# Start of a two-layer trunk: squares added by VectorE, projections in other PSUM banks, sinks on VectorE, modulation strips in front of their pair

## The chip, the cores and the metric

The kernel runs on one core of one Trainium2 chip. The time is the device time of one execution in microseconds (us). The kernel before was run three times: 1536.33, 1536.4 and 1539.2 us, median 1536.4 us. One further execution was profiled.

## The reference, cut to what matters

Two layers (DEPTH = 2) of a transformer-like trunk work on 512 latent tokens and 256 context tokens of width 1024. In each layer:

```python
h   = rmsnorm(x, norm1_g) * (1 + scale) + shift       # shift, scale = silu(c) @ w_mod + b_mod
z   = h @ w_in                                        # q 512, k 128, v 128, u 512, g 512 columns
q,k = rope(rmsnorm(q)), rope(rmsnorm(k))              # per head of 64; context without rope
attn = softmax(q k^T) v                               # 8 query heads, 2 key/value heads
gm   = gelu(u) * (w_spatial @ layernorm(gelu(g)) + b) # 128x128 mixing per chunk and group
x   += gate * (concat(attn, gm) @ w_out)
x   += gate * (square(relu(modulate(rmsnorm(x)) @ w_ff1)) @ w_ff2)
```

The context tokens use the same weights with a modulation of their own (c_ctx), and in the last layer only their keys and values are needed. Everything is float32 at the interface.

## The kernel before, in words

**Number format.** A float32 factor is split into a high part (rounded to the matmul type, by ScalarE, line 215) and a low part (the difference, by VectorE or GpSimd, line 216). A product takes three matmuls: high x high, high x low, low x high (`mm`, line 211). Activations are kept transposed, features on partitions, tokens along the free axis; `h0[k]` holds the high and low part of feature tile k (k = 0..7) for 768 tokens.

**Start.** `start` (lines 1183 to 1230) runs with the orders of TensorE (PE) and VectorE (DVE) written out by hand: the two engines execute its instructions in the order of the program. ScalarE (ACT) and GpSimd (POOL) are ordered by a planner before the run, and so is everything outside such a region. It works on the 512 latent tokens:

- The mean square per token: ACT squares each X[k] (line 1188), PE multiplies the 128x128 pieces of the square by a column of ones and accumulates over k (line 1192). Square tiles come from tag `s`, which has three buffers. VectorE scales, GpSimd takes the power -1/2 (line 292), VectorE spreads the result into a diagonal (`diag`, line 501), and four PE transposes turn it into a row for all partitions (`bcast`, line 506).
- Four modulation chunks (`mod_chunk`, lines 337 to 369), each in two halves of two 512 KB weight tiles and eight matmuls (line 348); here a half is called a strip. When a chunk is complete, VectorE transposes it in blocks (line 356), and its `fin` selects the rows with four matmuls (line 361) and stores shift and scale (`mod_store`, lines 421 and 424).
- For each pair of feature tiles c = 0..3: `convert` (lines 215 and 216) splits the projection weights of the pair, `pieces` (lines 494 to 496) makes `h0[2c]` and `h0[2c+1]` from X, scale, shift and the row of the norm, and `latents(k)` (line 598) multiplies them by 512 projection columns (keys, values and the first 256 queries): 12 matmuls for each k into four PSUM banks of tag `pa`. The strips of later chunks lie between and after the `latents` calls.
- The context's squares are added on GpSimd (`cx.step`, line 470); `cx.sums` stands in the middle of the last `latents` call. After `start` follow `cx.bcast()` and `cx.apply(h0)` (lines 1242 and 1243), which make the context's part of `h0`.

**DMA queue.** All weights are issued on SyncE's queue in the order of `block_order` (line 124): chunk 0, tok 0, chunk 1, tok 1, chunk 2, tok 2, chunk 3, tok 3, then the context's X and further weights. The first tiles land in buffers that are used again later (`EARLY`, line 119): chunk 2 goes where chunk 0 was, chunk 3 where chunk 1 was, so a load waits until the matmuls of the older chunk have read it.

**Projections of a layer.** `PLAN` (line 120) lists them: for layer 0 `w0` (gate u, tile 0, latent tokens), `kv` (sinks of what `start` has projected, then the context's projection in two banks of tag `pb`), `x0` (tile 0, context tokens), `u1`, then banks A0, u2, A1, A2, B0, B1, B2 (the spatial-gating part), then the second half of the queries and `u3`. `TokProj.bank` (line 553) computes 256 tokens by 256 columns: 48 matmuls into a PSUM bank, which its sink reads. PSUM has tags `pa` (two tiles of two banks), `pb` (two banks) and `pt` (two banks). The banks of `TokProj` come from `pt`, since `self.early` is true in both layers; `pt` also serves the mixing matmuls (line 853), the transposes of keys and queries (`turn`, line 724) and those of the norms.

**Sinks.** `both` (line 774) hands keys, values and first queries of 256 tokens to `sink_kv` and `sink_q`. Their `qk` (lines 678 to 707) squares on ACT, sums and multiplies by the rotary factors on VectorE, and, called with `pool` true, adds (line 696), takes the power (line 292) and multiplies (line 706) on GpSimd. `stack` (line 709) makes the low part on GpSimd in layer 0 (line 712), and `turn` transposes on PE. The gating sink `sink_g` runs gelu (lines 787 to 792), a layer norm and a mixing.

The later stages (attention, output projection, feed-forward) are not touched.

Of the kernel before, what the change touches and what calls it, by code (L numbers as in the profile page):

```python
# [15 lines left out]
D = 1024  # L16
# [152 lines left out]
def trunk(ctx: ExitStack, tc: tile.TileContext, xT, pk1, pk2, rope, wsT, w_mod, w_tok, w_u, w_out, w_ff1, w_ff2, outT):  # L169
# [57 lines left out]
    def convert():  # L227

        if held:
            split(*held.pop(0))  # L230
# [104 lines left out]
    fins = []  # L335

    def mod_chunk(l, j, lag=1200.0):
# [20 lines left out]
        def fin():  # L358
# [3 lines left out]
            mod_store(l, j, p4)  # L362
# [86 lines left out]
    class Norm:  # L449
# [22 lines left out]
        def sums(self, *others):  # L472
# [10 lines left out]
            r = rsqrt(v, o, self.l)  # L483
# [53 lines left out]
    class TokProj:  # L537
        def __init__(self, l, grp, h, npair, sink):
# [4 lines left out]
            self.early = PAR["BK"] == 1 and kv0 is None  # L543
# [122 lines left out]
    def layer(l, h, nxt, K, kv=None, kv0=0):  # L666
# [107 lines left out]
        def both(tp, ps):  # L774
            sink_kv(tp, [p[:, 0:256] for p in ps] if isinstance(ps, list) else ps[:, :, 0:256], True)
            q0(tp, [p[:, 256:512] for p in ps] if isinstance(ps, list) else ps[:, :, 256:512], True)
# [20 lines left out]
        def u_part(m, part):  # L797
# [5 lines left out]
            fm_mms(ps, w8(upart[m], h), off, n)  # L803
# [65 lines left out]
        with region('proj%d' % l):  # L869
            gproj = {}  # L870
            for s in PLAN[l]:
# [4 lines left out]
                elif s == "kv" and l == 0:  # L876
                    for tp in range(2):
                        both(tp, kv.ps[tp])
# [304 lines left out]
    def start():  # L1183
        ps = [pa() for _ in range(2)]
        chunk = [mod_chunk(0, c, None) for c in range(4)]
        for k in range(KT):
            sq = tsm([128, SEQ])
            act.activation(sq, xk(k)[:, 0:SEQ], AF.Square)
            if k == KT - 1:
                next(chunk[0])  # L1190
            for t in range(4):
                pe.matmul(ps[t // 2][:, t % 2 * 512:t % 2 * 512 + 1], sq[:, t * 128:(t + 1) * 128], ones[:, 0:1], start=k == 0, stop=k == KT - 1)  # L1192
        v = small(4)
        for i in range(2):
            vec.tensor_scalar(v[:, 2 * i:2 * i + 2], ps[i].rearrange("p (b n) -> p b n", b=2)[:, :, 0], 1.0 / D, EPS, op0=ALU.mult, op1=ALU.add)
        r = rsqrt(v, 4, 1)
        next(chunk[0])
        lat.diag(r)
# [4 lines left out]
        for c in range(4):  # L1203
            k = 2 * c
            lows = []
            if c:
                convert()
            lows.append(lat.pieces(h0, k))
# [6 lines left out]
            if c == 3:  # L1215
                convert()
                kvq.latents(k)
                kvq.latents(k + 1, cx.sums)
                break
# [3 lines left out]
            kvq.latents(k)  # L1223
            next(chunk[c + 1])
            kvq.latents(k + 1, lambda: fins.pop()())
            if c < 2:
                next(chunk[c + 2])
        P2 = K0[0]
        vec.tensor_scalar_mul(P2("bs"), P2("bs"), 0.5)
# [12 lines left out]
    cx.bcast()  # L1242
    cx.apply(h0)
# [63 lines left out]
```

## Time and profile before

| | us |
|---|---|
| median of three runs | 1536.4 |
| profiled execution, its own time | 1537.07 |
| its span | 1535.3 |
| PE busy in the span | 1478.6 (96%) |
| DVE / ACT / POOL busy | 882.3 / 638.7 / 360.8 |

The profiled execution lies 0.67 us over the median and 1.77 us over its own span. Times in the views are counted from the span's start. Engines: PE is TensorE (PEld its weight loads), DVE VectorE, ACT ScalarE, POOL GpSimd, SP SyncE. In a row of the timeline stand start, duration, engine, line, operation, output tile <- input tiles, shape, count and, in brackets, the idle time before it and what ended it. In a row of a view by stages each engine has its busy time with its count of instructions; then come the granted clock of PE (1.00 is full), the DMA share and the GB/s moved.

### The profile page before, as it was taken

What the parts mean: (1) busy time and instruction counts of PE and PEld (TensorE: products, weight loads), DVE (VectorE), ACT (ScalarE), POOL (GpSimd) and SP (SyncE); (2) the same over time, 40 slices, a digit from 0 to 9 for tenths busy, and PEclk for the clock granted to TensorE, in tenths of its full rate; (3) what the DMA queues carried; (4) which work ended last, traced back from release to release, by engine and by line L of the source; (5) the groups of instructions that cost most, each with busy time, mean ns of one, the idle gap of its engine ahead of it and who ended that gap; (6) DMA issues with size and microseconds to landing.
All of it is one profiled execution on the core that took longest, in us unless ns stands there. A gap on an engine that the chain in (4) does not pass through costs nothing.

```text
span 1535.3 us, 22099 instructions
## 1 busy us (share of the span) xinstructions
PE 1478.6 (96%) x8682; PEld 1297.0 (84%) x8682; DVE 882.3 (57%) x1593; ACT 638.7 (42%) x1081; POOL 360.8 (23%) x341
## 2 busy tenths in 40 slices
PE   7978989999999999999999999999999999999998
PEld 5668968788889898999999899898889888888887
DVE  2646676787855555444444446756795644444443
ACT  2443154665544543433333224534783433322221
POOL 0261240221244643213232303137113000000000
PEclk9999999999999999999999999998999999999999
DMA  8221164310143333333333321222101222233321
GB/s 326 95 70 54 56 233 152 112 42 15 49 129 121 117 117 117 117 105 122 110 124 113 107 69 42 77 75 69 42 1 56 97 96 96 96 96 97 99 97 65
DMA packets 50088, 148.78 MB, mean 97 GB/s; under 512 B 5440, under 2 KB 6976, under 8 KB 49984
## 3 DMA queue, kind: packets, MB, share of 16 engines
q1 hardware_dynamic: 49408, 146.72, 28.6%
q8 instruction: 68, 1.11, 0.3%
q10 hardware_dynamic: 576, 0.66, 0.1%
q14 instruction: 36, 0.29, 0.1%
HBM read 145.26 MB, written 2.10 MB: 96 GB/s over the span
## 4 chain that ended last, share of the span: by engine, by line
PE 83%; DVE 7%; ACT 4%; POOL 3%; issue 2%; DMA 1%; POOLq 0%; SPq 0%; ACTq 0%; DVEq 0%
PE pa L211 51%; PE pb L211 18%; PE pt L211 8%; PE pt L971 3%; PE pb L348 2%; POOL m L292 1%; PE pa L1192 1%; DVE lo L216 1%; PE pt L724 1%; ACT hi L215 1%; DVE A L513 1%; DVE X L911 1%; DVE s L517 1%; DVE B L1091 1%; ACT w L955 0%
## 5 line engine op out<-in xcount | busy, mean ns | idle before, releaser
L211 PE MATMUL pa<-A,hi 128*128 128x384 f32 (+2 forms) x1728 | 459.2, 348 | 3.4 <-ACT w L1084 1.0
L215 ACT CAST hi<-raw 128x1024 fp32r<-128x1024 f32 x168 | 176.5, 1051 | 450.7 <-PE pa L211 373.5
L211 PEld LDWEIGHTS pa<-A,hi 128*128 128x128 f32 x1728 | 310.7, 189 | 27.8 <-ACT w L1084 2.7
L216 DVE TENSOR_TENSOR lo<-raw,hi 128x1024 fp32r<-128x1024 f32 x152 | 194.2, 1277 | 237.3 <-ACT hi L215 233.9
L211 PE MATMUL pa<-A,lo 128*128 128x384 f32 (+2 forms) x864 | 299.2, 347 | 0.0
L211 PE MATMUL pa<-B,hi 128*128 128x512 f32 (+1 forms) x900 | 239.9, 355 | 3.6 <-DVE X L911 3.6
L394 POOL TENSOR_TENSOR C<-C,s 128x512 f32<-128x512 f32 x112 | 164.9, 1488 | 315.4 <-ACT s L393 273.5
L211 PEld LDWEIGHTS pa<-B,hi 128*128 128x128 f32 x900 | 158.8, 189 | 31.6 <-DVE X L911 5.9
L211 PEld LDWEIGHTS pa<-A,lo 128*128 128x128 f32 x864 | 162.8, 189 | 10.7
L911 DVE SCALAR_TENSOR_TENSOR X<-pa,modT,X 128x512 f32<-128x512 f32 x126 | 82.9, 660 | 141.1 <-PE pa L211 141.1
L211 PE MATMUL pb<-B,hi 128*128 128x512 f32 (+1 forms) x600 | 156.8, 350 | 2.0 <-DVE X L911 2.0
L211 PE MATMUL pa<-B,lo 128*128 128x512 f32 (+1 forms) x450 | 157.8, 355 | 0.0
L211 PE MATMUL pt<-hi,A 128*128 128x256 f32 x576 | 115.0, 297 | 8.2 <-DVE s L792 5.7
L211 PEld LDWEIGHTS pb<-B,hi 128*128 128x128 f32 x600 | 104.2, 189 | 16.5 <-DVE X L911 3.0
L911 DVE SCALAR_TENSOR_TENSOR X<-pb,modT,X 128x512 f32<-128x512 f32 (+3 forms) x116 | 71.0, 618 | 80.0 <-PE pb L211 79.7
L211 PEld LDWEIGHTS pt<-hi,A 128*128 128x128 f32 x576 | 97.0, 204 | 10.3 <-issue 7.8
L211 PE MATMUL pb<-B,lo 128*128 128x512 f32 (+1 forms) x300 | 104.6, 349 | 0.0
L393 ACT ACTIVATE s<-k,silu 128x512 f32<-128x512 f32 x112 | 76.8, 715 | 41.1 <-DMA k<-in_w_mod 31.6
L211 PEld LDWEIGHTS pa<-B,lo 128*128 128x128 f32 x450 | 84.1, 189 | 11.3
L211 PE MATMUL pt<-lo,A 128*128 128x256 f32 x288 | 84.9, 295 | 0.0
L974 DVE TENSOR_TENSOR A<-pt,A 128x384 fp32r<-128x384 f32 (+1 forms) x144 | 73.2, 535 | 10.3 <-ACT A L973 8.8
L973 ACT CAST A<-pt 128x384 fp32r<-128x384 f32 (+1 forms) x144 | 64.2, 469 | 31.0 <-PE pt L971 27.4
(195 smaller groups left out, 2242.7 us busy)
## 6 DMA issues: line engine op xcount, KB each, us to landing
raw<-in_w_ff SPq DMA_DIRECT2D x128, 512.0 KB, 3.5
k<-in_w_mod SPq DMA_DIRECT2D x96, 256.0 KB, 3.1
raw<-in_w_tok SPq DMA_DIRECT2D x16, 512.0 KB, 3.5
raw<-in_w_out SPq DMA_DIRECT2D x16, 512.0 KB, 3.5
lo<-in_w_mod SPq DMA_DIRECT2D x16, 512.0 KB, 4.7
hi<-in_w_mod SPq DMA_DIRECT2D x16, 512.0 KB, 4.4
A<-in_w_mod SPq DMA_DIRECT2D x8, 512.0 KB, 6.8
B<-in_w_mod SPq DMA_DIRECT2D x8, 512.0 KB, 7.8
```

The source lines that it names most:

```text
L211: pe.matmul(out, a, b, start=start, stop=stop)
L215: act.copy(hi, src)
L216: (eng or vec).tensor_tensor(out=lo, in0=src, in1=hi.bitcast(F32), op=ALU.subtract)
L292: pool_e.tensor_tensor(out=y, in0=v, in1=mhalf[:, 0:n], op=ALU.pow)
L348: pe.matmul(ps[q:q + 32, :], S32[:, k, :], ws_[k2 // 2][:, k2 % 2 * 512:(k2 % 2 + 1) * 512], start=k < ns, stop=k >= KT - ns)
L393: act.activation(p, w, AF.Copy, scale=s)
L394: pool_e.tensor_tensor(out=a, in0=a, in1=p, op=ALU.add)
L513: (pool_e if k % 2 < PAR['LP'].get('%d%d%d' % (l, w, off // 256), 0) else vec).scalar_tensor_tensor(out=h[k][:, 1, off:off + n], in0=t, sc ...
L911: vec.scalar_tensor_tensor(out=xs, in0=src[:, s - off:e - off], scalar=modT[l][:, i * 8 + m, cond:cond + 1], in1=xs, op0=ALU.mult, op1=ALU ...
L971: pe.transpose(tp_[:, (kt - k0) * 128:(kt - k0) * 128 + 128], p[:, kt * 128:kt * 128 + 128], ident)
L973: act.copy(pth[:, k0:k0 + step, d], src)
L974: vec.tensor_tensor(out=ptl[:, k0:k0 + step, d], in0=src, in1=pth[:, k0:k0 + step, d].bitcast(F32), op=ALU.subtract)
```

## The change

- The squares of the latent tokens are no longer multiplied by ones tile by tile. `lat.step(k)` squares on ACT and adds on VectorE; `lat.sums(pool=1)` multiplies the finished sum by ones once (four matmuls). It stands behind chunk 0, whose two strips now run one after the other (`run(chunk[0])`).
- In the loop over pairs, both strips of chunk c + 1 run directly in front of `latents(2c)` for c = 1 and 2 (chunk 1: its first strip before the loop, its second between the two `latents` of c = 0). The selecting matmuls of a chunk stand in the middle of a `latents` call of the pair before the one that uses the chunk; `mod_store` of chunks 1 to 3 is put off (`mods`) until behind the next `convert`.
- `cx.bcast()` stands inside `w0`, behind the matmuls of k = 4, in an order of PE written out by hand, and `cx.apply(h)` behind its matmuls; before, both stood in front of `w0`. The halving of the spatial bias moves behind `start`.
- `both` calls the sinks without `pool`: addition, inverse square root (nine small operations, lines 295 to 305) and product run on VectorE in layer 0. `stack` stays on GpSimd.
- `self.early` is false: the banks of `TokProj` come from `pb` in both layers.

```diff
--- before.py
+++ after.py
@@ -332,7 +332,7 @@
     modT = [const.tile([128, 48, 2], F32, name=f"modT{l}") for l in range(DEPTH)]
     Amod = [[const.tile([128, 8, 2], F32, name=f"A{l}{w}") for w in range(2)] for l in range(DEPTH)]
 
-    fins = []
+    fins, mods = [], []
 
     def mod_chunk(l, j, lag=1200.0):
 
@@ -359,7 +359,10 @@
             p4 = pt((128, 4, 2))
             for a in range(4):
                 pe.matmul(p4[a * 32:a * 32 + 32], P1("sel")[0:rows], tr[0:rows].rearrange("p (m a i) -> p a m i", m=4, a=4)[:, a, :, 0:2], start=True, stop=True)
-            mod_store(l, j, p4)
+            if l == 0 and 0 < j < 4:
+                mods.append(lambda: mod_store(l, j, p4))
+            else:
+                mod_store(l, j, p4)
         if lag is None:
             fins.append(fin)
         elif lag:
@@ -469,7 +472,7 @@
             eng = pool_e if k < 7 and PAR["NP"] & self.tagn or self is cx else vec
             eng.tensor_tensor(out=self.acc, in0=self.acc, in1=sq, op=ALU.add)
 
-        def sums(self, *others):
+        def sums(self, *others, pool=0):
 
             every = (self,) + others
             ps = pt()
@@ -480,7 +483,7 @@
                     o += 1
             v = small(o)
             vec.tensor_scalar(v, ps[:, 0:o], 1.0 / D, EPS, op0=ALU.mult, op1=ALU.add)
-            r = rsqrt(v, o, self.l)
+            r = rsqrt(v, o, self.l or pool)
             o = 0
             for a in every:
                 a.diag(r[:, o:o + a.n // 128])
@@ -540,7 +543,7 @@
             self.key = ("tok", l, grp)
             self.l, self.grp = l, grp
             self.wb = {}
-            self.early = PAR["BK"] == 1 and kv0 is None
+            self.early = False
 
         def passes(self, k):
             if k // 4 not in self.wb:
@@ -772,8 +775,8 @@
         q0 = sink_q(0)
 
         def both(tp, ps):
-            sink_kv(tp, [p[:, 0:256] for p in ps] if isinstance(ps, list) else ps[:, :, 0:256], True)
-            q0(tp, [p[:, 256:512] for p in ps] if isinstance(ps, list) else ps[:, :, 256:512], True)
+            sink_kv(tp, [p[:, 0:256] for p in ps] if isinstance(ps, list) else ps[:, :, 0:256])
+            q0(tp, [p[:, 256:512] for p in ps] if isinstance(ps, list) else ps[:, :, 256:512])
         if kv is None:
             kv = TokProj(l, 0, h, 3, None)
             kv.sink = sink_kv
@@ -800,7 +803,16 @@
             if part == 0:
                 upart[m] = take("u", l, m)
             ps = pt()[:, 0:n]
-            fm_mms(ps, w8(upart[m], h), off, n)
+            if part:
+                fm_mms(ps, w8(upart[m], h), off, n)
+            else:
+                with tc.manual_schedule(engines={mybir.EngineType.PE}):
+                    for k, (whi, wlo, rhi, rlo) in enumerate(w8(upart[m], h)):
+                        for i, (a, b) in enumerate(((whi, rhi), (whi, rlo), (wlo, rhi))):
+                            mm(ps, a, b[:, off:off + n], k == 0 and i == 0, k == KT - 1 and i == 2, n)
+                        if k == 4:
+                            cx.bcast()
+                cx.apply(h)
             if part:
                 release()
             fl.tick()
@@ -874,6 +886,7 @@
                 elif s[0] in "wx":
                     u_part(int(s[1]), "wx".index(s[0]))
                 elif s == "kv" and l == 0:
+                    vec.tensor_scalar_mul(P2("bs"), P2("bs"), 0.5)
                     for tp in range(2):
                         both(tp, kv.ps[tp])
                     both(2, kv.context())
@@ -1181,52 +1194,38 @@
             steady(range(8))
 
     def start():
-        ps = [pa() for _ in range(2)]
         chunk = [mod_chunk(0, c, None) for c in range(4)]
         for k in range(KT):
-            sq = tsm([128, SEQ])
-            act.activation(sq, xk(k)[:, 0:SEQ], AF.Square)
-            if k == KT - 1:
-                next(chunk[0])
-            for t in range(4):
-                pe.matmul(ps[t // 2][:, t % 2 * 512:t % 2 * 512 + 1], sq[:, t * 128:(t + 1) * 128], ones[:, 0:1], start=k == 0, stop=k == KT - 1)
-        v = small(4)
-        for i in range(2):
-            vec.tensor_scalar(v[:, 2 * i:2 * i + 2], ps[i].rearrange("p (b n) -> p b n", b=2)[:, :, 0], 1.0 / D, EPS, op0=ALU.mult, op1=ALU.add)
-        r = rsqrt(v, 4, 1)
-        next(chunk[0])
-        lat.diag(r)
+            lat.step(k)
+        run(chunk[0])
+        lat.sums(pool=1)
         fins.pop()()
         lat.bcast()
         next(chunk[1])
         kvq = WideProj(h0)
         for c in range(4):
             k = 2 * c
-            lows = []
             if c:
                 convert()
-            lows.append(lat.pieces(h0, k))
+                mods.pop()()
+            lows = [lat.pieces(h0, k)]
             if not c:
                 convert()
                 lows.pop()()
             lows.append(lat.pieces(h0, k + 1))
             for f in lows:
                 f()
-            if c == 3:
-                convert()
-                kvq.latents(k)
-                kvq.latents(k + 1, cx.sums)
-                break
             if c == 2:
                 for i in range(KT):
                     cx.step(i)
-            kvq.latents(k)
-            next(chunk[c + 1])
-            kvq.latents(k + 1, lambda: fins.pop()())
-            if c < 2:
-                next(chunk[c + 2])
-        P2 = K0[0]
-        vec.tensor_scalar_mul(P2("bs"), P2("bs"), 0.5)
+            if c == 3:
+                convert()
+            if 0 < c < 3:
+                run(chunk[c + 1])
+            kvq.latents(k, fins.pop() if fins else None)
+            if not c:
+                run(chunk[1])
+            kvq.latents(k + 1, cx.sums if c == 3 else fins.pop() if fins else None)
         return kvq
 
     k2s = [const.tile([128, 640], F32, tag="k2", name=nm("k2"))]
@@ -1239,8 +1238,6 @@
     while held:
         convert()
     held = None
-    cx.bcast()
-    cx.apply(h0)
     h1, K1 = [], []
     layer(0, h0, h1, K0, kvq)
     layer(1, h1, None, K1[0])
```

## The prediction

> **What bounds the kernel now.** I read the page's busy times and chain of waits first.
>
> ```profile
> PE 1478.6 (96%) x8682; PEld 1297.0 (84%) x8682; DVE 882.3 (57%) x1593; ACT 638.7 (42%) x1081; POOL 360.8 (23%) x341
> PE 83%; DVE 7%; ACT 4%; POOL 3%; issue 2%; DMA 1%; POOLq 0%; SPq 0%; ACTq 0%; DVEq 0%
> ```
>
> TensorE bounds the run. The change takes little work from it, so it can gain only where PE idles or runs slowly, 1535.3 - 1478.6 = 56.7 us of idle time. The view by stages says where (cut at the start, the context's norm, the projections of layer 0 in two parts, those of layer 1):
>
> ```profile
> 0.00:57.50 57.50, 45.82 (x237) 29.30 (x237) 21.83 (x48) 17.69 (x30) 7.54 (x14) 1.00 0.72 262
> 57.50:65.00 7.50, 6.59 (x29) 4.88 (x30) 5.28 (x16) 2.06 (x3) 0.00 (x0) 1.00 0.41 141
> 65.00:117.00 52.00, 41.37 (x219) 36.37 (x220) 28.59 (x62) 25.99 (x54) 25.68 (x22) 0.95 0.19 61
> 117.00:206.00 89.00, 81.63 (x608) 76.92 (x609) 60.26 (x216) 25.08 (x44) 19.76 (x17) 0.95 0.22 80
> 960.00:1060.00 100.00, 94.09 (x635) 87.80 (x634) 63.28 (x150) 43.86 (x74) 40.76 (x33) 0.93 0.22 70
> ```
>
> Idle PE in the four stages up to 206 us: 11.7 + 0.9 + 10.6 + 7.4 = 30.6 us, and 5.9 us in the fifth: two thirds of all idle time lies where the change is made. The granted clock of 0.95, 0.95 and 0.93 costs another 0.05 x 52 = 2.6, 0.05 x 89 = 4.5 and 0.07 x 100 = 7 us. The view of waits names the causes, first for the whole run, then for layer 1's projections:
>
> ```profile
> PE pt L724 <- POOL k L712: 8.7, 3, 4.9
> PE pt L211 <- DVE s L792: 6.0, 4, 2.8
> ...
> PE pt L211 <- DVE s L859: 2.1, 2, 1.1
> PE pt L724 <- DVE s L859: 1.1, 1, 1.1
> PE pt L211 <- DVE m L704: 0.9, 1, 0.9
> ```
>
> The transposes of keys and queries wait for GpSimd (8.7), and projection banks of tag `pt` wait for gelu's last reader (6.0): the change touches both.
>
> **Part 1, up to the first projection matmul.**
>
> ```profile
> 7.68 12.07 PE L1192 MATMUL pa<-ones,s 128*128 128x1 f32 x56 [7.68 <-ACT s L1188]
> 17.85 1.04 ACT L215 CAST hi<-B 128x1024 fp32r<-128x1024 f32 x1 [0.78 <-DMA B<-in_w_tok]
> 19.69 1.93 PE L348 MATMUL pb<-A,S 128*32 128x512 f32 x8
> 21.55 1.87 PE L1192 MATMUL pa<-ones,s 128*128 128x1 f32 x8
> 23.76 1.02 POOL L292 TENSOR_TENSOR m<-m,mhalf 128x4 f32<-128x4 f32 x1 [22.78 <-DVE m L1195]
> ...
> 26.45 1.12 PE L506 MATMUL pt<-c,w 128*128 128x128 f32 x4
> 27.67 0.75 DVE L494 SCALAR_TENSOR_TENSOR s<-X,A,pt 128x512 f32<-128x512 f32 x1 [0.80 <-PE pt L506]
> ...
> 29.36 0.54 PE L211 MATMUL pa<-hi,A 128*128 128x512 f32 x1
> ...
> 60.21 0.69 DVE L216 TENSOR_TENSOR ws<-raw,ws 128x512 fp32r<-128x512 f32 x1
> ```
>
> Now PE itself paces the squares: 64 records for eight of them, the last ending at 23.42, with chunk 0's first strip wedged in at 19.69. In the change VectorE adds seven squares at the 0.69 of the L216 row (same shape, two SBUF inputs), 4.8 us while X arrives, on an engine that idles there; PE's part shrinks to the 1.87 us of the second L1192 row (the same eight records). What is late next is chunk 0's load.
>
> ```profile
> GB/s 0 35 287 175 260 326 328 406 401 406 420 410 414 406 414 410 406 414 410 410 406 393 180 254 414 356 86 377 397 438 291 184 373 410 127 172 356 418 397 384
> ```
>
> This is the DMA rate in slices of 1 us. Ahead of chunk 0's last tile stand 0.36 MB of constants, 2.10 MB of X and 2.10 MB of the chunk, 4.55 MB; the slices reach that at 14.7 us. The tok load behind it (5.07 MB, 16.0 us by the slices) was seen by ACT at 17.85, some 1.8 us later, so I put the chunk at 16.4. Then: second strip 1.93, to 18.35; sums 1.87, to 20.2; scaling and handing over 0.35 (from L1192's end 23.42 to 23.76); power 1.02, to 21.6; diagonal 0.45; transposes at 22.1; L494 1.22 later; the first matmul another 1.69 later, at 25.0. The first strip of chunk 1 stands between, as now. **-4.4 us** against 29.36. Bounds: -2.9 if the chunk lands only with tok (17.85), -6.1 if at 14.7. As chunk 0's buffers come free 7 us earlier, chunk 2's load starts behind tok 1 without the holes of the GB/s row at slices 23 and 27; by the same count it is there at about 29, chunk 3 at 36.
>
> A matter of warmth: the strip at 19.69 takes 1.93 after 12 us of L1192 matmuls, the same strip takes 1.06 at 32.79 (row below), with the granted clock at 1.00 for both. So these matmuls don't speed PE up, and leaving them out costs nothing here. The Trainium skill, page "TensorE: Matmul & The Clock Gate", section "Part 1: The HAM clock gate", says that TensorE runs at half clock until it has been busy for about 3.4 us. By that rule the removed matmuls would be a warm-up, and the sum 2 x 0.87 = 1.7 us worse; the 1.93 after 12 us speaks against it.
>
> **Part 2, the four pairs.**
>
> ```profile
> 32.79 1.06 PE L348 MATMUL pb<-B,S 128*32 128x512 f32 x8
> 35.38 0.25 PE L361 MATMUL pt<-w,c 128*32 128x8 f32 x8
> 57.49 0.50 PE L211 MATMUL pa<-hi,A 128*128 128x512 f32 x1 [1.93 <-ACT A L495]
> ...
> 62.59 0.16 DVE L482 TENSOR_SCALAR m<-pt 128x2 f32<-128x2 f32 x1 [1.69 <-PE pt L479]
> 64.56 0.29 DVE L501 COPY w<-m 128x256 f32<-128x256 f32 x1
> 63.65 0.40 PE L211 MATMUL pa<-hi,A 128*128 128x512 f32 x1
> 64.91 0.44 PE L506 MATMUL pt<-c,w 128*128 128x128 f32 x2 [0.86 <-DVE w L501]
> 65.10 0.71 PE L211 MATMUL pt<-A,hi 128*128 128x512 f32 x2
> 68.21 0.48 DVE L517 SCALAR_TENSOR_TENSOR s<-X,A,pt 128x256 f32<-128x256 f32 x1
> 69.00 0.48 DVE L517 SCALAR_TENSOR_TENSOR s<-X,A,pt 128x256 f32<-128x256 f32 x1
> ```
>
> From 29.36 to 64.05 PE takes 34.7 us. Its work: the last 24 matmuls take 64.05 - 57.49 = 6.56, less 0.49 of waiting for the low part and 0.57 for the sums, so 0.229 each; 96 x 0.229 = 22.0. Five strips at 1.0, three selections at 0.33, the sums 0.57: 28.6. The rest, 6.1, is waiting: the store comes out of the middle of the second `latents`, then 1.2 us of conversion and `pieces` follow on VectorE while at most one strip fills PE. In the change a chunk is selected a whole `latents` earlier (except chunk 1), and two strips and one `latents` lie ahead of its use, about 4 us, against a DVE chain of 0.3 + 2.9 us from store to low parts, the conversion already done ahead of it. I leave 1.3 us for the first pair: 29.9, **-4.8 us**; bounds -1.9 (only the longest wait goes) and -6.1. The loads have 2 to 5 us to spare: chunk 2 is used at 33, chunk 3 at 41.
>
> **Part 3, the context's row.** `w0` follows at 64.05 + 1.05 now. Behind k = 4 of `w0` the transposes have 15 x 0.229 = 3.4 us of cover for a chain of 2.3 us (from L482 to L501's end); 0.44 stays. **-0.6 us.** `cx.apply` starts later against `w0`'s end by 3.4 us, but the context's projection needs one piece per 6 x 0.229 = 1.4 us and VectorE makes one per 0.8 (the two L517 rows). If that cover fails, 1 us.
>
> Parts 1 to 3: **-9.8 us**, bounds -5.4 and -12.8.
>
> **Part 4, layer 0's projections.** Sinks: GpSimd loses additions, powers and products, VectorE gets them.
>
> ```profile
> 74.39 0.74 POOL L696 TENSOR_TENSOR w<-w,s 128x256 f32<-128x256 f32 x1 [17.78 <-DVE m L704]
> 82.73 2.22 POOL L696 TENSOR_TENSOR w<-w,s 128x512 f32<-128x512 f32 x1 [3.70 <-DVE m L704]
> 113.59 1.30 POOL L712 TENSOR_TENSOR k<-w,k 128x512 fp32r<-128x512 f32 x1 [3.83 <-ACT k L711]
> ...
> L696 DVE TENSOR_TENSOR w<-w,s 128x512 f32<-128x512 f32 x2 | 1.4, 689 | 0.0
> L758 DVE TENSOR_TENSOR B<-pa,B 128x256 fp32r<-128x256 f32 x2 | 0.8, 414 | 0.0
> 187.64 0.17 DVE L295 TENSOR_SCALAR m<-m 128x8 int32<-128x8 int32 x1
> ...
> 189.25 0.17 DVE L305 SCALAR_TENSOR_TENSOR m<-m,m 128x8 f32<-128x8 f32 x1
> ```
>
> The second half of the queries does this on VectorE already: 0.69 for 128x512, 1.8 us for the nine operations from L295 to L305. Added: four additions (2 x 0.69 + 2 x 0.41), six inverse roots (10.8), six products (3 x 0.69 + 3 x 0.41): 16.3 us. The chain of six sinks on GpSimd now runs from 74.4 to 114.9. On VectorE the six need, with their sums and rotary products, some 28 us, and the conversions and gelus between them 10: the last transpose comes hardly earlier, those before it do. Queued behind each of these operations are gelu, which frees banks, and the conversion of weights. Of the 8.7 us I take half, -4.4. Banks: with `pb` for projections and `pt` for mixing and transposes, a bank has 5.8 us (a whole bank of matmuls) to be read instead of none, but the context's projection holds both `pb` banks until VectorE has read them: of the 6.0 us I take -4.0. Half of the lost clock, -3.5, goes with the gaps. Against that VectorE gets to (28.59 + 60.26 + 16.3) / 131 = 80% load over the stage, so a fifth of what is added meets a busy engine on PE's path: +3.3. Sum **-8.6 us**. Bounds: -22 (all waits and clock), and +14: all 16.3 on the path, 8.7 saved, and the six L712 of GpSimd (6.0 us) in VectorE's way. That the two slow each other shows in 2.22 us for the addition at 82.73, three times that at 74.39 for twice the columns. The Trainium skill, page "SBUF — State Buffer", section "SBUF: two separate sides", has a rule for it: a VectorE operation with two SBUF inputs and a GpSimd operation that reads SBUF hold a shared pair of ports by turns, each for its whole length. By it the move ends more collisions than it makes; the trace fits, and the bound is kept.
>
> **Part 5, layer 1.** Only the banks change: 4.1 us of waits and 7 us of clock can go, but `u0`, `u1` and nine banks share two `pb`. I take **-3 us**; bounds -11 and +3 (one gelu wait like the longest, 2.8). Feed-forward and attention shift unchanged.
>
> **Sum.** -9.8 - 8.6 - 3.0 = -21.4; 1537.07 - 21.4 = **1515.7 us**. The profiled execution lies 0.67 over the median of 1536.4.
>
> **The rivals.** *Start alone:* the planner puts transposes and banks as late as now, since VectorE's sinks end as late as GpSimd's; 1537.1 - 9.8 = 1527.3. For it speaks the equal length of the two chains, against it that `pt` is free of banks. *All gaps close:* layer 0 gives 18, layer 1 gives 7: 1502.3. For it speaks PE's 0.95 clock, which recovers with the gaps; against it the 80% of VectorE. *VectorE becomes the bound, slower:* its sinks hold PSUM banks `pa` and `pb` so long that PE stands. Price: +14 in layer 0, less 9.8: 1541.3. It decides once more than 9.8 us beyond today's waits of layer 0 land on PE. For it: six inverse roots of nine operations in a row; against it: VectorE idles 23 of 52 us between 65 and 117. *The change does not do what it says:* strips wait for loads in front of the pair instead of behind it, and the sinks eat the rest; about 1537.
>
> **Numbers.** Forecast 0.50 (own range 1507 to 1524), start alone 0.24, all gaps 0.12, slower 0.11, nothing 0.03. A difference of 0.2%, 3 us, can be told from none. Faster: 0.50 + 0.23 + 0.12 = 0.85; same 0.04; slower 0.11. The range 1502 to 1535 holds the forecast, nearly all of "start alone" and half of "all gaps"; left out are slower and the best end.
>
> **What would show it.** First L211 near 25 us; last `latents` matmul near 55; no wait of L211 for L495 after the first pair; the waits for L712 halved or replaced by ones for VectorE; waits of `pt` for L792 gone; clock near 1.00 from 117 to 206. Wrong if PE waits for `in_w_mod` in front of a pair, if the context's banks keep PE from bank A0, or if VectorE is near full with PE idle between 60 and 110.

## The result and the profile after

| | median us (runs) | lowest to highest |
|---|---|---|
| before | 1537.14 (6) | 1533.89 to 1539.2 |
| changed | 1511.21 (6) | 1506.11 to 1512.62 |

The ratio is 0.9825, with a 95% interval of 0.9805 to 0.9844: the change makes the kernel 1.75% faster. The forecast was 1516 us, the range 1502 to 1535. The profiled execution of the changed kernel took 1506.11 us with a span of 1504.3; it is the fastest of the six. Against the profiled execution before, 31.0 us are gone from the span; by the medians it is 25.9.

The first two rows are the busy times and the chain of waits of the changed kernel.

```profile
PE 1453.5 (97%) x8626; PEld 1276.9 (85%) x8626; DVE 898.4 (60%) x1663; ACT 638.6 (42%) x1081; POOL 345.5 (23%) x325
PE 82%; DVE 7%; ACT 4%; POOL 3%; issue 2%; DMA 2%; SPq 0%; POOLq 0%; ACTq 0%; DVEq 0%
```

TensorE is still the bound. Its idle time fell from 56.7 to 50.8 us and its busy time by 25.1. Of these, 12.9 are the matmuls by ones that are left out (12.07 + 1.87 before, 1.05 now); the other 12.2 are matmuls that take less time, so gaps that are gone are the smaller part of the gain. An estimate from the mean granted clock of the two executions, 0.990 and 0.995, puts some 8 of the 12.2 us down to the clock (0.010 x 1535.3 less 0.005 x 1504.3). The view by stages, with the same columns as in the prediction, shows where.

```profile
0.00:57.50 57.50, 43.30 (x237) 27.23 (x238) 35.73 (x76) 21.00 (x35) 8.45 (x14) 1.00 0.74 280
65.00:117.00 52.00, 46.06 (x318) 43.16 (x318) 42.82 (x149) 25.70 (x52) 7.55 (x7) 1.00 0.19 62
65.00:80.00 15.00, 11.35 (x69) 10.12 (x68) 14.32 (x50) 7.36 (x15) 0.76 (x1) 1.00 0.44 141
80.00:95.00 15.00, 13.52 (x87) 12.15 (x88) 14.41 (x55) 8.25 (x21) 4.16 (x4) 1.00 0.01 2
117.00:206.00 89.00, 78.39 (x571) 68.36 (x570) 60.57 (x207) 31.47 (x64) 30.00 (x27) 0.92 0.36 125
920.00:1020.70 100.70, 99.50 (x744) 94.72 (x743) 73.94 (x166) 48.05 (x83) 40.29 (x30) 1.00 0.26 79
```

Layer 0: from 65 to 117 us VectorE went from 28.59 to 42.82 us of work and GpSimd from 25.68 to 7.55. From 65 to 95 VectorE is full (14.32 and 14.41 of 15) while TensorE idles 5.1 us, against 3.0 before; the view of waits of this stretch lists 3.2 us for VectorE (L698) and 1.2 for GpSimd (L715). The clock is 1.00 up to 117, and 0.92 after it. Layer 1's projections are the last row. The same stretch of work before is this one:

```profile
941.00:1054.00 113.00, 106.45 (x745) 100.34 (x744) 73.66 (x167) 48.43 (x83) 39.63 (x34) 0.94 0.23 71
1040.00:1050.00 10.00, 8.72 (x40) 8.59 (x41) 3.28 (x8) 0.60 (x1) 9.84 (x8) 0.50 0.18 63
```

745 matmuls before and 744 after: 6.55 us of idle time became 1.2, and the busy time of the same work fell by 6.95 as the clock rose from 0.94 to 1.00. The second row is the worst piece of the old stage, with a clock of 0.50.

The view of waits of the changed kernel (engine, tile and line that wait, what they wait for, sum, times, longest):

```profile
PE pb L348 <- DMA A<-in_w_mod: 11.6, 1, 11.6
PE pt L211 <- ACT B L215: 5.6, 1, 5.6
...
PE pa L211 <- DVE s L698: 3.2, 2, 2.4
...
PE pt L727 <- POOL k L715: 2.5, 4, 0.8
PE pb L211 <- POOL A L915: 2.4, 2, 2.1
PE pa L211 <- DVE s L795: 2.2, 1, 2.2
```

The transposes' wait for GpSimd fell from 8.7 to 2.5. The waits of tag `pt` for gelu (6.0) are gone; one of 2.2 is left, of tag `pa`. Three waits of some size are new: 5.6 us in front of a mixing (for the high part of the layer norm's output), 3.2 for rotary products, and 2.4 in the last layer's output projection.

The timeline gives the stage boundaries (columns as in the prediction).

```profile
11.57 4.80 PE L348 MATMUL pb<-A,S 128*32 128x512 f32 x16 [11.57 <-DMA A<-in_w_mod]
16.30 1.05 PE L482 MATMUL pt<-ones,acc 128*128 128x1 f32 x8
...
19.88 1.06 PE L348 MATMUL pb<-B,S 128*32 128x512 f32 x8
21.55 0.50 PE L211 MATMUL pa<-hi,A 128*128 128x512 f32 x1 [0.60 <-ACT A L498]
...
51.17 0.62 PE L211 MATMUL pt<-A,hi 128*128 128x512 f32 x2
54.60 0.38 PE L509 MATMUL pt<-c,w 128*128 128x128 f32 x2
55.08 1.26 DVE L520 SCALAR_TENSOR_TENSOR s<-X,A,pt 128x256 f32<-128x256 f32 x3 [2.94 <-PE pt L509]
...
154.82 0.69 PE L211 MATMUL pt<-ws,B 128*128 128x128 f32 x2 [5.55 <-ACT B L215]
1020.77 0.95 PE L211 MATMUL pa<-B,B 128*128 128x512 f32 x4
1025.44 0.50 PE L211 MATMUL pb<-A,hi 128*128 128x512 f32 x1 [2.10 <-POOL A L915]
```

In the table, each stage runs from one first matmul to the next: of the projections of `start` (21.55), of `w0` (51.17), of attention in layer 0, of layer 1's projections, of layer 1's attention (1020.77), of layer 1's feed-forward.

| stage, us | before | changed | difference |
|---|---|---|---|
| up to the first projection matmul | 29.4 | 21.6 | -7.8 |
| the four pairs, up to `w0` | 35.7 | 29.6 | -6.1 |
| layer 0's projections | 132.1 | 125.0 | -7.1 |
| layer 0's attention | 190.4 | 190.0 | -0.4 |
| layer 1's projections | 112.4 | 100.6 | -11.8 |
| layer 1's attention | 147.5 | 149.7 | +2.2 |

They sum to -31.0, the whole difference of the spans; the rest of the run is equal.

### The profile page after: what moved, and what is told of

The parts are those of the page before. It is cut to its first block, busy times and chain, and to the rows that moved or that the text cites. A ratio compares the mean times of both kernels' runs of the same rounds, so it can differ in the third digit from the quotient of the medians.

```text
span 1504.3 us, 22027 instructions
## 1 busy us (share of the span) xinstructions
PE 1453.5 (97%) x8626; PEld 1276.9 (85%) x8626; DVE 898.4 (60%) x1663; ACT 638.6 (42%) x1081; POOL 345.5 (23%) x325
## 3 DMA queue, kind: packets, MB, share of 16 engines
q1 hardware_dynamic: 49408, 146.72, 29.5%
## 4 chain that ended last, share of the span: by engine, by line
PE 82%; DVE 7%; ACT 4%; POOL 3%; issue 2%; DMA 2%; SPq 0%; POOLq 0%; ACTq 0%; DVEq 0%
PE pa L211 53%; PE pb L211 21%; PE pt L984 3%; PE pt L211 2%; PE pb L348 2%; POOL m L292 1%; DVE lo L216 1%; ACT hi L215 1%; DMA A<-in_w_mod 1%; DVE X L924 1%; DVE s L851 1%; DVE B L1104 1%; PE pt L727 1%; POOL lo L216 1%; DMA k<-in_pk 0%
## 5 line engine op out<-in xcount | busy, mean ns | idle before, releaser
L211 PEld LDWEIGHTS pa<-A,lo 128*128 128x128 f32 x864 | 162.9, 189 | 10.7
L211 PE MATMUL pb<-hi,A 128*128 128x256 f32 (+1 forms) x608 | 119.1, 292 | 0.1
L211 PEld LDWEIGHTS pb<-hi,A 128*128 128x128 f32 x608 | 98.0, 193 | 1.8 <-DVE w L703 0.4
L211 PE MATMUL pb<-lo,A 128*128 128x256 f32 (+1 forms) x304 | 88.4, 291 | 0.0
L968 ACT ACTIVATE w<-pa,m 128x768 f32<-128x768 f32 (+1 forms) x80 | 65.7, 822 | 30.7 <-DVE m L965 28.8
```

Of the source, the lines that this page charges most:

```text
L211: pe.matmul(out, a, b, start=start, stop=stop)
L968: act.activation(p, ps[:, 0:nk], AF.Exp, bias=nmx, accum_out=sm)
```

## The experiments

The theory was that the gain adds up from three parts that work for the reasons given: the start (squares and strips), the banks, the sinks. The rivals differ from run to run and stand in the expectations. Each ratio below is to runs of the kernel before on the same chip. The chips differ from run to run (the kernel before took 1537.1 to 1539.2 us on them, by medians), so where two intervals overlap, a difference of medians is no more than a hint. Diffs are against the changed kernel where nothing else is said. The stages of all runs are in a table at the end of this section.

**The start alone:** banks and sinks as before.

```diff
-            self.early = False
+            self.early = True          # and True again as last argument of both sinks in `both`
```

> The changed start and context row alone; sinks on GpSimd and projection banks of tag pt as before. Theory (the three parts add up): w0 begins at 51 instead of 65 us, layer 0's projections and layer 1 keep their waits, so some 14 us off: 1523. Rival (the start's gain is given back, since the transposes wait for GpSimd's chain whatever begins earlier): 1531 to 1537.

Measured: 1526.5 us, ratio 0.9922 (0.9905 to 0.9938). Nearer to the theory, but 11 us instead of 14: the start gives 11.9 in its own two stages (29.4 to 23.4, 35.7 to 29.8; `w0` begins at 53.2, not 51), and layer 0's projections give 3.6 back (135.7). The old waits are all there (6.5 us of `pt` for gelu's L795, 7.5 for GpSimd's L715), and one of 2.9 us for the rotary products (L698) is new: TensorE comes earlier, its suppliers do not.

**The banks alone,** against the kernel before:

```diff
-            self.early = PAR["BK"] == 1 and kv0 is None
+            self.early = False
```

> The kernel before with the projection banks in pb, nothing else. Theory: layer 1's projections lose their waits for pt and the slow clock behind them, 8 to 12 us, and layer 0 loses part of the 6 us of waits for gelu, so 1523 to 1528. Rival (layer 1's gain in the changed kernel's profile was one execution's luck with the clock): 1532 to 1537, with layer 1's projections as long as before.

Measured: 1522.85 us, ratio 0.9903 (0.9888 to 0.9917). The theory holds. Layer 1's projections take 100.7 us instead of 112.4, layer 0's give 3.5, and layer 1's attention loses 2.4, as in the full change. The row of its view by stages for layer 1's projections has the idle time and the clock of the changed kernel:

```profile
937.00:1037.50 100.50, 99.29 (x743) 94.48 (x742) 73.69 (x166) 47.87 (x82) 40.32 (x30) 1.00 0.25 80
```

**The sinks alone,** against the kernel before: both sinks without `True`.

> The kernel before with the sinks of keys and first queries on VectorE, banks still in pt. Theory (the transposes' 8.7 us of waits for GpSimd go, VectorE's added 16 us take part of that back): 1530 to 1535. Rival (VectorE becomes the bound of layer 0 when nothing else is changed): 1538 to 1543. Rival (the sinks are the larger part of layer 0's gain): below 1528.

Measured: 1533.3 us, ratio 0.9974 (0.9965 to 0.9983). The theory holds: 3.9 us, of which 3.7 in layer 0's projections. The wait for GpSimd falls from 8.7 only to 5.8 here.

**Banks back, sinks back,** one at a time in the changed kernel:

```diff
-            self.early = False
+            self.early = True
```

> The changed kernel with projection banks back in pt in both layers. Theory: layer 1 as long as before (10 us more than in the changed kernel), layer 0 a few us longer: 1522 to 1527. Rival (banks are worth little once the sinks are on VectorE): 1511 to 1516.

```diff
-            sink_kv(tp, [p[:, 0:256] for p in ps] if isinstance(ps, list) else ps[:, :, 0:256])
+            sink_kv(tp, [p[:, 0:256] for p in ps] if isinstance(ps, list) else ps[:, :, 0:256], True)
...
+            q0(tp, ..., True)
```

> The changed kernel with the sinks of keys and first queries back on GpSimd. Theory (after the runs so far: start 11, banks 14.5, sinks 4 us of 26, sinks worth 1 us once start and banks are changed): 1511 to 1514, transposes waiting for GpSimd again in layer 0. Rival of the prediction (half of 8.7 us of waits plus their clock come back): 1516 to 1519.

Measured: banks back 1525.1 us, ratio 0.9915 (0.989 to 0.9939): the theory holds, with layer 1's projections at 109.6 and layer 0's at 132.6. The waits of `pt` for gelu are back at 6.0 us. Sinks back 1514.6 us, ratio 0.9835 (0.9816 to 0.9854): between theory and rival, and its interval overlaps that of the change. In its profile layer 0's projections take 6.5 us longer and the wait for GpSimd is back; by the medians the sinks are worth 3.4 us, and that is not told apart from none.

```profile
PE pt L727 <- POOL k L715: 6.8, 6, 2.7
PE pt L211 <- ACT B L215: 5.6, 1, 5.6
```

The 5.6 us in front of the mixing is the same with either engine: the sinks did not make it. It stands in the run with the banks alone too (5.5 in two waits, the longer 5.2).

**Squares back on TensorE,** all else as changed: does the start gain from leaving out 56 slow matmuls, and were they a warm-up?

```diff
-            lat.step(k)
+            sq = tsm([128, SEQ])
+            act.activation(sq, xk(k)[:, 0:SEQ], AF.Square)
+            for t in range(4):
+                pe.matmul(ps[t // 2][:, t % 2 * 512:t % 2 * 512 + 1], sq[:, t * 128:(t + 1) * 128], ones[:, 0:1], start=k == 0, stop=k == KT - 1)
         run(chunk[0])
```

> The changed kernel with the squares multiplied by ones on PE as before, both strips of chunk 0 behind them as in the change. Theory (the matmuls with one column pace the start and do not speed PE up): first projection matmul at 26 to 28 us instead of 21.5 to 23.5, strips of chunk 0 at 1.9 us each, total 1514 to 1517. Rival (they are a warm-up: the strips run at 1.06 us each right behind them): strips at 1.06 us, first projection matmul at 24 to 25.

Measured: 1516.0 us, ratio 0.985 (0.9822 to 0.9878). As the theory has it, the strips do not speed up: 3.64 us for the two of chunk 0, 1.94 for that of chunk 1, behind 13.8 us of unbroken one-column matmuls.

```profile
6.96 13.78 PE L1203 MATMUL pa<-ones,s 128*128 128x1 f32 x64 [6.96 <-ACT s L1201]
20.67 3.64 PE L348 MATMUL pb<-A,S 128*32 128x512 f32 x16
...
27.96 1.94 PE L348 MATMUL pb<-B,S 128*32 128x512 f32 x8
29.83 0.58 PE L211 MATMUL pa<-hi,A 128*128 128x512 f32 x1
```

Both strips stand behind all 64 matmuls here, so the first projection matmul is at 29.8, later than the 26 to 28 expected. The interval overlaps that of the change: what is shown is the stage, not the total. The other stages stay within 3.1 us of the changed kernel's, of both signs.

**Strips back:** the order of strips, selections and stores as before, the rest as changed.

```diff
+            mod_store(l, j, p4)             # at once, none put off
...
-            if 0 < c < 3:
-                run(chunk[c + 1])
-            kvq.latents(k, fins.pop() if fins else None)
-            if not c:
-                run(chunk[1])
-            kvq.latents(k + 1, cx.sums if c == 3 else fins.pop() if fins else None)
+            kvq.latents(k)
+            if c == 3:
+                kvq.latents(k + 1, cx.sums)
+                break
+            next(chunk[c + 1])
+            kvq.latents(k + 1, lambda: fins.pop()())
+            if c < 2:
+                next(chunk[c + 2])
```

> The changed kernel with the strips of chunks 1 to 3 and their stores placed as before (squares stay on VectorE). Theory (the prediction's part 2: the order alone is worth 4.8 us, the waits for scale and pieces in front of each pair return): from the first projection matmul to w0 34 to 36 us instead of 29.6, total 1515 to 1518. Rival (the waits before came from the late loads, which the earlier start has removed): 30 to 31 us, 1511 to 1513.

Measured: 1514.7 us, ratio 0.9843 (0.9828 to 0.9858). The four pairs take 34.8 us instead of 29.6, and the wait of `latents` for the pieces is back. The theory holds for the stage; of its 5.2 us the medians show 3.5, and the intervals overlap. The first matmul, the first one of `w0`, and then the wait from the view of waits:

```profile
21.99 0.51 PE L211 MATMUL pa<-hi,A 128*128 128x512 f32 x1 [0.60 <-ACT A L495]
...
56.80 0.62 PE L211 MATMUL pt<-A,hi 128*128 128x512 f32 x2
```

```profile
PE pa L211 <- ACT A L495: 3.5, 4, 2.0
```

**The context's row in front of `w0` again.** In the changed kernel VectorE stands still for 2.94 us until the row is there (L520 at 55.08 in the timeline above), and from 65 to 95 it is full.

```diff
-                        if k == 4:
-                            cx.bcast()
-                cx.apply(h)
...
     held = None
+    cx.bcast()
+    cx.apply(h0)
```

> The changed kernel with the context's row and its pieces in front of w0 again. Theory (0.6 us of PE's waiting come back, nothing else moves): w0 starts 1.0 to 1.3 us later, total 1511 to 1513. Rival (the pieces that start 3.4 us earlier relieve VectorE in layer 0's projections): below 1510.

Measured: 1505.5 us, ratio 0.9779 (0.9761 to 0.9796), clear of the change's interval. The rival holds: this part of the change is a loss. Timeline, then stages of this run:

```profile
53.67 0.71 PE L211 MATMUL pt<-A,hi 128*128 128x512 f32 x2
54.02 1.26 DVE L520 SCALAR_TENSOR_TENSOR s<-X,A,pt 128x256 f32<-128x256 f32 x3 [0.60 <-PE pt L509]
```

```profile
65.00:80.00 15.00, 15.00 (x91) 13.78 (x90) 14.76 (x48) 8.04 (x15) 0.81 (x2) 1.00 0.46 146
80.00:95.00 15.00, 12.81 (x87) 11.64 (x86) 12.37 (x50) 8.33 (x21) 3.98 (x4) 1.00 0.08 31
```

VectorE begins the context's pieces 0.35 us after `w0` starts instead of 3.9. TensorE pays 1.1 us in front of `w0` and gets 3.9 in the projections (121.1): from 65 to 80 it idles not at all, instead of 3.65 us, and the wait for the rotary products (L698, 3.2 us) is gone. That is 2.8 us of the 5.7 between the medians. The rest stays open: the profiled execution of the change was its fastest, and four of its six runs, with a whole-run clock of 0.989 to 0.991 against 0.994 to 0.995 in the two profiled executions, have no profile. As an estimate, 0.004 of the clock over 1505 us is up to 6 us, so the clock may hold the rest.

**GpSimd's part in the norm and in the output projection.** The layer norm's power goes to GpSimd, and in the last layer the low part of the gated product goes to VectorE.

```diff
-                r = rsqrt(ve, 4, l)
+                r = rsqrt(ve, 4, 1)
...
-                (pool_e if g > 1 else vec).tensor_tensor(out=gm[:, 1, 0:TQ], ...
+                (pool_e if g > 1 and not last else vec).tensor_tensor(out=gm[:, 1, 0:TQ], ...
```

> The changed kernel with two further moves: the inverse root of the gating's layer norm in layer 0 on GpSimd instead of nine operations of VectorE, and the low parts of the gated tiles in the last layer on VectorE instead of GpSimd. Theory (VectorE's chain of layer norm is what layer 0's projections wait for now, 5.6 us at 154.82, and GpSimd's queue what the last layer's attention waits for, 2.4 us): layer 0's projections 3 to 6 us shorter, the last layer's attention 2 us shorter, total 1503 to 1507. Rival (the planner's other order eats it, or GpSimd's power of 1.0 to 2.0 us is as slow as the chain of 1.8): 1509 to 1513.

Measured: 1506.0 us, ratio 0.9783 (0.9764 to 0.9801). The total is as the theory has it, but not for the reason given in layer 0: its projections did not shorten (125.5 against 125.0) and the wait in front of the mixing is still 4.8 us. The profile can't say more of the first edit, since from 65 to 95 us, ahead of the layer norms, its clock is 0.89 against 1.00 in the change. The second edit did what it should: layer 1's attention takes 147.8 instead of 149.7, and its 2.4 us wait for L915 is gone. That is 1.9 of the 5.2 us between the medians; the rest is as open as in the run before this one.

**Both good edits together:** the row in front of `w0` (e10 in the expectations) and the last layer's low part on VectorE (from the run just above, e11); the new version is e12.

> The changed kernel with the context's row in front of w0 again (as in e10) and the low parts of the gated tiles in the last layer on VectorE (as in e11). Theory (the two act in different stages and add up: layer 0's projections 4 us shorter than in the change, the last layer's attention 2 us): 1502 to 1505. Rival (e10's gain was one planner's order by luck): 1506 to 1510.

Measured: 1503.1 us (1501.93 to 1504.34), ratio 0.9767 (0.9751 to 0.9783). The theory holds by stages: layer 0's projections take 121.5 instead of 125.0 and layer 1's attention 147.6 instead of 149.7. This is the lowest median of the study, 2.3% under the kernel before; its interval overlaps that of the run with the row alone.

**Half of the sinks back to GpSimd,** from that version: keys and values, then first queries.

```diff
+            sink_kv(..., True)          # the first of the two runs
+            q0(..., True)               # the second
```

> e12 with the sinks of keys on GpSimd and those of the first queries on VectorE. Theory (VectorE is what layer 0's projections wait for between 65 and 95 us, so sharing the sinks relieves it by 7 us of work): layer 0's projections 1 to 4 us shorter than in e12, 1500 to 1503. Rival (GpSimd's chain is long again and the transposes wait for it): 1504 to 1509.

> e12 with the sinks of the first queries on GpSimd and those of keys on VectorE. Theory (as for e13, 9 us of work leave VectorE): 1500 to 1504. Rival (GpSimd's products of 128x512 at 1 to 2.4 us make its chain longer than with keys alone): 1505 to 1510.

Measured: 1506.4 us, ratio 0.9789 (0.9774 to 0.9804), and 1509.0 us, ratio 0.9804 (0.9787 to 0.9822). The theory fell, both are slower than the version they start from (on the same chip it took 1501.9 to 1504.3 us, these two 1506.0 to 1507.3 and 1508.7 to 1510.0). Layer 0's projections take 3.0 and 5.4 us longer. In the first, a wait of 3.1 us of a projection for VectorE's L707 appears; in the second, the transposes wait for GpSimd once more:

```profile
PE pt L727 <- POOL k L715: 6.7, 4, 3.8
```

So VectorE, full as it is, is still the better place for each of the two.

| run | to first proj. | pairs | layer 0 proj. | layer 0 att. | layer 1 proj. | layer 1 att. |
|---|---|---|---|---|---|---|
| before | 29.4 | 35.7 | 132.1 | 190.4 | 112.4 | 147.5 |
| changed | 21.6 | 29.6 | 125.0 | 190.0 | 100.6 | 149.7 |
| start alone | 23.4 | 29.8 | 135.7 | 191.5 | 110.5 | 147.5 |
| banks alone | 28.5 | 38.2 | 128.6 | 187.7 | 100.7 | 149.9 |
| sinks alone | 28.4 | 37.5 | 128.4 | 190.8 | 112.2 | 147.4 |
| banks back | 23.6 | 29.7 | 132.6 | 193.2 | 109.6 | 147.6 |
| sinks back | 22.9 | 29.4 | 131.5 | 190.2 | 100.6 | 151.2 |
| squares back | 29.8 | 29.5 | 128.1 | 188.3 | 100.7 | 151.5 |
| strips back | 22.0 | 34.8 | 126.5 | 190.2 | 100.7 | 149.7 |
| row in front | 23.0 | 30.7 | 121.1 | 189.9 | 100.7 | 149.7 |
| norm's power, low part | 22.6 | 29.5 | 125.5 | 189.6 | 100.7 | 147.8 |
| row and low part | 23.4 | 30.7 | 121.5 | 190.0 | 100.7 | 147.6 |
| same, keys on GpSimd | 23.0 | 30.7 | 124.5 | 190.1 | 100.7 | 147.6 |
| same, queries on GpSimd | 23.2 | 30.7 | 126.9 | 190.7 | 101.8 | 147.1 |

By medians the three parts alone give 10.7, 14.3 and 3.9 us, 28.8 together; the change gives 25.9. They add up but for some 3 us, and the largest is the banks, an edit of one line.

## Why the prediction was right, and where it was not

The forecast of 1516 lies 5 us above the median. The mechanism was right: the start, the pairs, both projections and nothing else that gains. The sizes were not all right, and one term had the wrong sign.

**Part 1** said -4.4 with bounds to -6.1; the profile shows -7.8. Two steps were mis-sized. "I put the chunk at 16.4" let the second strip begin only with the last tile: TensorE began on the chunk's first tiles at 11.57, was busy almost without a break, and both strips were through at 16.4, where I had 18.35. And the strips and the sums were put in with times of the kernel before, in which TensorE ran at half speed (see the next paragraph): the sums took 1.05 instead of 1.87. The two make 2.0 and 0.8 of the 3.4 us missed. Part of the 7.8 is this one execution (its strip of chunk 1 took 1.06, in eight of the others 1.94): in the other runs of this start the first matmul is at 22.0 to 23.6, and the starts of before, banks alone and sinks alone lie between 28.4 and 29.4. By the means of these groups it is about -5.9. By the medians, squares back on TensorE cost 4.8 us, with intervals that overlap.

**Warmth.** (The prediction's word for whether earlier matmuls speed up later ones.) That leaving out the ones-matmuls costs no speed was right: behind 13.8 us of them strips take as long as behind 12 (1.82 and 1.93 each). The Trainium skill, page "TensorE: Matmul & The Clock Gate", section "Part 1: The HAM clock gate", would have had them at full speed by then; the measurement decides. What does not hold is "with the granted clock at 1.00 for both". A trace lists the clock in entries; that of the kernel before has none ahead of 29.48 us, and a view prints 1.00 where there is none. The single matmuls of the strips (mean in ns behind the busy time) show the speed: the kernel before from 19.6 to 29.3 and at 32.8 us, then the changed kernel from 11.5 to 13.5 and from 15.0 to 16.2.

```profile
L348 PE MATMUL pb<-A,S 128*32 128x512 f32 x16 | 3.9, 1059 | 0.0
L348 PE MATMUL pb<-B,S 128*32 128x512 f32 x8 | 1.1, 604 | 0.0
...
L348 PE MATMUL pb<-A,S 128*32 128x512 f32 x6 | 2.3, 1056 | 11.6 <-DMA A<-in_w_mod 11.6
L348 PE MATMUL pb<-A,S 128*32 128x512 f32 x6 | 1.6, 601 | 0.1
```

The changed kernel's first entry, of 1.00, lies at 14.38 us, between its two rows. In the ten profiles with the squares on VectorE it lies at 14.4 to 18.2 us, in the four with the ones-matmuls at 29.5 to 31.3. So the change brings full speed some 14 us earlier, which the prediction did not price.

The early strip of chunk 1 follows the clock as well: in the eight profiles in which it takes 1.94 us the clock has fallen back to 0.50 by then, in the change (1.06) and in "strips back" (1.07) it has not. From 20 to 22 us, the run with the row in front and then the change:

```profile
20.00:22.00 2.00, 1.90 (x12) 0.91 (x12) 0.97 (x4) 0.00 (x0) 0.00 (x0) 0.50 1.02 408
20.00:22.00 2.00, 1.40 (x10) 0.30 (x8) 2.00 (x3) 0.72 (x1) 0.00 (x0) 1.00 1.04 416
```

Why it falls back in eight of the ten is open.

**Part 2** said -4.8, with a bound of -6.1. From the first matmul to `w0` it is -6.1, and with the row's 1.05 of before taken out -5.1. Putting the order back costs 5.2. This term is right, 0.3 off. That it fits so closely is partly luck: with the banks alone and the sinks alone the same pairs, which those edits do not touch, took 38.2 and 37.5 us instead of 35.7, with the same waits and a clock of 0.96 and 0.95 instead of 1.00.

**Part 3** said -0.6 and "if that cover fails, 1 us". TensorE's own gain is there, 1.1 us. The step that failed is that a later `cx.apply` is harmless since "the context's projection needs one piece per 1.4 us and VectorE makes one per 0.8". That counted one consumer. The sinks, gelu and weight conversions queue behind the pieces on VectorE, which is full up to 95 us; 2.94 us in which it stands still for the row come out behind them. The sign was wrong: with the row in front the kernel is 5.7 us faster by the medians, of which the stages of the two profiles show 2.8.

**Part 4** said -8.6; it is -7.1. The sum is close, its terms less so.

- Half of the waits for GpSimd was taken, 4.4; 6.2 of 8.7 went, though with the sinks alone only 2.9.
- 4.0 of 6.0 for the `pt` banks was taken; all of that tag went, 2.2 came back at `pa`.
- The clock was to gain 3.5 and to be near 1.00 from 117 to 206; it is 0.92. Clock 1.00 came in the stage up to 117 (0.95 before), and was lost from 150.9 to 161.1, around the 5.6 us wait that ends at 154.82, which was not foreseen. As this wait is there with the banks alone and with the sinks back, and in no run with the banks in `pt`, the banks bring it out.
- VectorE's load over the stage was to be 80%; from 51.17 to 176.17 it is 79% (98.74 of 125 us), but from 65 to 95 it is 96%, and TensorE idles 5.1 us there. A mean over the stage hid that, and "a fifth of what is added meets a busy engine" does not follow from it: at 80% a fifth is the idle share. The prediction had named VectorE near full with PE idle as a sign of being wrong, and the rival *VectorE becomes the bound* had the right place and the wrong price: with the sinks back on GpSimd it is no faster.
- The term was also put on the wrong parts of the sum: banks and sinks alone give 3.5 and 3.7, and the start alone takes 3.6.

**Part 5** said -3 with a bound of -11; it is -11.8. The mis-sized step is to take less than half of "4.1 us of waits and 7 us of clock", because two `pb` banks would be short. They are not: all idle time but 1.2 us and all of the slow clock went. The banks alone show the same.

**"Feed-forward and attention shift unchanged"** missed 2.2 us in layer 1's attention. The projections now end so early that GpSimd's low part (L915), hidden before, is late for the output projection; the run with that part on VectorE shows it.

**The rivals.** *Start alone* (1527.3) priced the run with the start alone well (1526.5), but the rest did not stay at nothing. *All gaps close* was nearer for layer 1 (-7 against -11.8 measured) and far off for layer 0 (-18 against -7.1). *No change* fell: no strip waits for a load in front of its pair.

**Total.** Measured less predicted, between the two profiled executions: -3.4 (part 1), -0.7 (parts 2 and 3, 6.1 against 5.4), +1.5 (part 4), -8.8 (part 5), +1.8 (attention in both layers, -0.4 and +2.2); together -9.6, which is 31.0 less 21.4. The errors of opposite sign hide little. That the forecast lies only 5 us above the median, and not 9.6, is luck: the profiled execution was 5.1 us under the median.

## What to carry to other kernels

Layer 1's projections, a stage in which many short waits went together with a granted clock under 1.00, were worth their waits and their whole loss of clock; layer 0's were not, since new waits took the place of the old. So price both as one, and look first for the few banks or buffers that cause them. Before delaying the input of an engine, count everything that is queued behind it in the window in which that engine is full; a mean load over a longer stage hides that window. After a gain, look at what was hidden by the time that is now gone: here GpSimd's low part in the last attention and the wait in front of the mixing.

## What the runs showed of the hardware

**A clock of 0.50 with no long wait.** In the kernel before, from 1040 to 1050 us, TensorE was busy 8.72 of 10 us, and the view of waits lists two there, 2.1 us in all (the prediction's row for L859), the longer 1.1 us. The granted clock was 0.50. With the banks in `pb` the stage is at 1.00. So here gaps of about 1 us went with half a clock. The fall begins at 1039.83; the view of waits lists 0.9 us in the 3.4 us ahead of it, yet TensorE was busy for only 1.88 of 3.43:

```profile
1036.40:1039.83 3.43, 1.88 (x15) 1.56 (x14) 1.79 (x6) 0.04 (x1) 3.43 (x3) 1.00 0.35 103
```

All entries of the clock but the last of each of the 14 traces last 3.41 us or a multiple of it. Cut into steps of 3.41 us, every step at full clock with TensorE busy under 44% was followed by a fall to 0.50, and none with TensorE busy over 72%; between the two it went either way (29 falls in 81 steps). So in these traces the fall goes with the sum of the gaps in a step, and no single long wait is needed.

**VectorE and GpSimd in each other's way.** Three of the small operations of the inverse roots, now on VectorE, stretch beside GpSimd's subtraction of 512 or 256 columns. The timeline of the changed kernel:

```profile
80.64 1.40 POOL L715 TENSOR_TENSOR k<-w,k 128x512 fp32r<-128x512 f32 x1 [5.89 <-ACT k L714]
80.83 1.23 DVE L301 TENSOR_TENSOR m<-m 128x4 f32<-128x4 f32 x1
82.28 0.15 DVE L302 TENSOR_TENSOR m<-m,m 128x4 f32<-128x4 f32 x1
...
84.98 0.74 POOL L715 TENSOR_TENSOR k<-w,k 128x256 fp32r<-128x256 f32 x1 [2.94 <-ACT k L714]
85.10 0.64 DVE L301 TENSOR_TENSOR m<-m 128x8 f32<-128x8 f32 x1
...
89.85 1.28 POOL L715 TENSOR_TENSOR k<-w,k 128x512 fp32r<-128x512 f32 x1 [4.12 <-ACT k L714]
89.96 1.19 DVE L302 TENSOR_TENSOR m<-m,m 128x4 f32<-128x4 f32 x1
```

An operation on four columns takes 0.15 us alone and 1.23 behind GpSimd's 1.40: each of the three ends within 0.02 us of GpSimd's operation. Together they cost the full VectorE 2.6 us. This agrees with the Trainium skill, page "SBUF — State Buffer", section "SBUF: two separate sides", by which the two hold a port pair by turns, each for its whole operation.
